# Experts of a large and a small group in alternation, in an encoder trunk on one core

## The chip, the cores and the metric

The kernel runs on 1 core of one Trainium2 chip. The metric is the device time of one execution in microseconds; the median of three runs is 1874.84 us (1874.23 to 1879.55). All computation uses five engines with their own instruction queues: TensorE (PE, matrix products into PSUM), VectorE (DVE), ScalarE (ACT), GpSimd (POOL) and SyncE (SP, which issues the transfers here). An engine takes its instructions strictly in the order in which they stand in its queue.

## The reference

Two layers of an encoder on 512 frames of width 1024. Each layer has a mixer part (retention, differential attention, gated linear attention; not touched here) and then a mixture of experts. The experts are 32 SwiGLU blocks of inner width 512, in 8 groups of 4. A router gives each frame one group and, in it, two experts:

```python
grp = biased.reshape(t, N_GROUPS, EXPERTS_PER_GROUP)
group_score = jnp.sum(lax.top_k(grp, GROUP_SCORE_K)[0], axis=-1)
g_sel = jnp.argmax(group_score, axis=-1)
...
u = jax.nn.silu(xb @ w_gate[e]) * (xb @ w_up[e])
return (u @ w_down[e]) * gts[:, None].astype(xb.dtype)
...
x = x + gt2 * y
```

Everything is float32. The weights of one expert are three matrices of 2 MiB (gate 1024x512, up 1024x512, down 512x1024), so a layer reads 192 MiB of them from HBM.

## The kernel before

The groups are ranked by how many frames chose them. The first four ranks ("wide", `r < NWIDE`) get 128 places each, the last four ("small") 64. All four experts of a group work on all of its places, with gate weights of zero where a frame has not chosen the expert. (Frames that find no place go through a loop behind, which doesn't run for these inputs unless a group overflows.)

Weights come in pieces of 1 MiB (128 partitions x 8 KiB), two to a matrix, issued by SyncE (`fetch`, line 1436) into eight rotating buffers (tag `R8`, names R in the trace; `oldest` picks the place that was used longest ago). A buffer can take its next piece when its last reader is done. What reads it depends on the kind of expert:

- Wide: `split` (line 1407) makes two fp32r halves of each half-piece, ScalarE a rounded copy (`A.copy`, CAST H<-R) and VectorE the rest (`V.tensor_sub`, H<-R,H), into six rotating buffers (tag `H8`, names H). PE multiplies three times per block of the contraction (`three`, line 1417), with 128x128 tiles and 512 columns. The R buffer is free as soon as it is split.
- Small: PE multiplies the float32 piece as it landed (`halved`, line 1421) with 128x64 tiles, and the R buffer stays taken until then.

For expert e the program writes, in this order: the gate product of expert e+1 (`gate_part`; in its middle, `turn` transposes the inner result u of expert e on PE, with ScalarE and VectorE writing the turned copy euT), the down product of e (`down_part`), and the up product of e+1 (`up_part`, whose end is the VectorE multiplication that writes eu). `_Ahead` lets the fetches and splits be written four half-pieces ahead of their use. In this stage every VectorE, ScalarE, GpSimd and TensorE instruction keeps the order in which it is written (`_Pinned`, line 111).

Two further steps belong to a group. `window` (line 1369) makes a wide group's input columns xT (exT) as fp32r pairs, one ScalarE copy and one VectorE subtraction of 128x1024; there is one buffer for it. `combine` (line 1574) adds a finished group's sums to the frames: a mask (ePT) and for each half of the width a gain (eyf), its two fp32r parts (eyh), PE products back to the frame order (x<-eyh,ePT) and a VectorE addition (u<-u,x). It is a generator: `step` (line 1459), called once after each half-piece that PE has multiplied, writes its next portion, so that it runs among the products of later experts. The sums of a wide group take two PSUM banks (tag `y`), those of a small one another bank (tag `y64`, also shown as y in the trace).

What sets the order of the experts is the table `TURNS` (line 35) and the list `where` (line 1588): (rank, number in the group) of the 32 experts; the fetches follow it. Before, the groups come as wholes: the four experts of wide group 0, the four of small group 4, then 1, 5, 2, 6, 3, 7. One variable `ya` holds the sums of the open group.

Of the kernel before, what the change touches and what calls it, by code (L numbers as in the profile page):

```python
# [23 lines left out]
NE, NG, FE = 32, 8, 512  # L24
# [5 lines left out]
NWIDE = 4  # L30
# [1 line left out]
OFFS = tuple(sum(CAPS[:r]) for r in range(NG))  # L32
PLACES = sum(CAPS)

TURNS = (0, 4, 1, 5, 2, 6, 3, 7)


def _constants():
# [100 lines left out]
def hybrid_trunk(ctx: ExitStack, tc: tile.TileContext, x, c, positions, w_mod, b_mod, norm1_g, norm2_g, w_in,  # L139
# [52 lines left out]
    def preload(name):  # L192

        tables[0] = tc.keep_in_program_order(A.preload_act_table_set(name))
# [156 lines left out]
    for l in range(depth):  # L351
        first = l == 0
        with ExitStack() as ps:
# [997 lines left out]
            def pbank(tag, bufs=1, shape=None):  # L1351
                return pm.tile(shape or [128, 512], tag=tag, bufs=bufs)
# [16 lines left out]
            def window(r):  # L1369

                nwin[0] += 1
                xT = wm.tile([128, 2, KD, 128], F32R, tag="exT")
                w = slice(OFFS[r], OFFS[r] + 128)
                for h in ((0, 4), (4, 8)) if nwin[0] == 1 else ((0, 8),):
                    ks = slice(*h)
                    A.copy(xT[:, 0, ks], hs[:, ks, w])
                    V.tensor_sub(xT[:, 1, ks], hs[:, ks, w], xT[:, 0, ks])
                return xT
# [3 lines left out]
            def back(r):  # L1382

                PT = wm.tile([128, NT, 128], F32R, tag="ePT")
                V.tensor_scalar(PT.rearrange("p i t -> p (i t)"), srow, cst("scol")[:, r:r + 1], None, op0=OP.is_equal)
                return PT
# [30 lines left out]
            def three(out, a, ka, hl, c0, start, stop):  # L1417
                for n, (x_, w_) in enumerate(((0, 0), (0, 1), (1, 0))):
                    T.matmul(out, a[:, x_, ka], hl[:, w_, c0:c0 + 512], start=(start and n == 0), stop=(stop and n == 2))

            def halved(out, a, raw, c0, n, start, stop):

                n //= 2
                for h in range(2):
                    T.matmul(out[64 * h:64 * h + 64, 0:n], a, raw[:, c0 + h * n:c0 + (h + 1) * n], start=start, stop=stop)
# [31 lines left out]
            apart = deque()  # L1457

            def step():

                if apart and next(apart[0], apart) is apart:
                    apart.popleft()
# [32 lines left out]
            def turn(u_, e):  # L1495
                b = pbank("x", 3, [128, 4, 128])
                if where[e][0] < NWIDE:
                    for q in range(4):
                        T.transpose(b[:, q], u_.rearrange("p (q t k) -> p q k t", q=2, k=2)[:, q // 2, q % 2], ident)
                    uT = wm.tile([128, 2, 4, 128], F32R, tag="euT")  # L1500
                    A.copy(uT[:, 0], b)
                    V.tensor_sub(uT[:, 1], b, uT[:, 0])
                else:
                    for k in range(2):
                        T.transpose(b[:, k], u_.rearrange("p (t k) -> p k t", k=2)[:, k], ident)
                    uT = wm.tile([128, 2, 128], tag="euT64")
                    A.copy(uT, b[:, 0:2])
                return uT

            def down_part(src, e, uT, ya, amid=None):  # L1510
                r, j = where[e]
                for k in range(4):
                    hl = src.get()
                    start, stop = j == 0 and k == 0, j == 3 and k == 3
                    if r < NWIDE:
                        for n in range(2):
                            three(ya[:, n], uT, k, hl, n * 512, start, stop)
                    else:
                        halved(ya[:, 0], uT[:, k % 2, 64 * (k // 2):64 * (k // 2) + 64], hl, 0, D, start, stop)
                    step()  # L1520
                    if amid and k == 1:
                        amid()

            def gain_y(ya, n, yf, wide_):
                V.tensor_mul(yf, ya[:, n], after["gt2b"][:, n * 512:(n + 1) * 512] if wide_ else after["gt2h"])
                return yf

            def gated(ya, n, wide_):
                return parts(gain_y(ya, n, after["pool"].tile([128, 512], tag="eyf"), wide_))

            def parts(yf):
                yh = after["pool"].tile([128, 2, 512], F32R, tag="eyh", bufs=2)
                A.copy(yh[:, 0], yf)
                V.tensor_sub(yh[:, 1], yf, yh[:, 0])
                return yh

            def store(i, cs_=slice(0, D)):
                SP.dma_start(out[0, i * 128:(i + 1) * 128, cs_], X[:, i, cs_])

            def squares(i, n):  # L1540
                A.activation(wm.tile([128, FE], tag="es"), X[:, i, n * 512:(n + 1) * 512], AF.Square,
                             accum_out=sums[:, i, n:n + 1])

            def add(PT, yhs, ns, i):

                if len(yhs) == 2:
                    bs = [(n, pbank("x", 3), slice(0, 128), yhs[n]) for n in ns]
                else:
                    bs = [(n, pbank("x", 3), slice(64 * n, 64 * n + 64), yhs[0]) for n in ns]
                for m in range(2):  # L1550
                    for n, b, rows, yh in bs:
                        T.matmul(b, PT[rows, i], yh[rows, m], start=(m == 0), stop=(m == 1))
                for n, b, rows, yh in bs:
                    V.tensor_add(X[:, i, n * 512:(n + 1) * 512], X[:, i, n * 512:(n + 1) * 512], b)

            def combine_last(r, ya):

                wide_ = r < NWIDE
                if l + 1 < depth:
                    preload("natural_log_exp_and_others")  # L1560
                PT = back(r)
                yfs = [gain_y(ya, n, wm.tile([128, 512], tag=("es", "eu")[n]), wide_) for n in range(2 if wide_ else 1)]
                yhs = [parts(yf) for yf in yfs]
                for i in range(NT):
                    add(PT, yhs, (0, 1), i)
                    if l + 1 < depth:
                        for n in range(2):
                            squares(i, n)
                    else:
                        store(i)  # L1570
                if l + 1 < depth:
                    row_rstd()

            def combine(r, ya):

                PT = back(r)
                yield
                yhs = []
                for n in range(2 if r < NWIDE else 1):
                    yhs.append(gated(ya, n, r < NWIDE))  # L1580
                    yield
                for ns in ((0,), (1,)) if r < NWIDE else ((0, 1),):
                    for i in range(NT):
                        add(PT, yhs, ns, i)
                        yield


            where = [(r, j) for r in TURNS for j in range(4)]
            ne = len(where)
            items = halves_of(w_gate, 0) + halves_of(w_up, 0)  # L1590
            for e in range(ne):
# [1 line left out]
                mine = halves_of(w_down, e)  # L1593
                items += nxt_[0] + (mine + nxt_[1] if e + 2 < ne else nxt_[1] + mine)
            src = _Ahead(pieces(items), lambda: 4)
            xTs = {TURNS[0]: window(TURNS[0])}

            gh = rt.tile([128, 2, NT, 4], F32R)
            V.tensor_copy(gh[:, 0], gate4)
# [33 lines left out]
            def sums_bank(r):  # L1633
                return pbank("y", 1, [128, 2, 512]) if r < NWIDE else pbank("y64", 1, [128, 1, 512])

            ya = sums_bank(TURNS[0])
            V, A, G, T = [_Pinned(tc, e_) if n_ in "VAGT" else e_ for n_, e_ in
                          (("V", nc.vector), ("A", nc.scalar), ("G", nc.gpsimd), ("T", nc.tensor))]
            turned = []
            for e in range(ne):  # L1640
                r, j = where[e]
                if j == 2 and e + 2 < ne and where[e + 2][0] < NWIDE:
                    xTs[where[e + 2][0]] = window(where[e + 2][0])
                uT = []
                if e + 1 < ne:
                    gacc = gate_part(src, e + 1, lambda: uT.append(turn(u_, e)))
                elif not turned:
                    uT.append(turn(u_, e))
                if e + 2 == ne:

                    u2 = up_part(src, e + 1, gacc)
                    down_part(src, e, uT[0], ya, lambda: turned.append(turn(u2, e + 1)))
                    continue
                down_part(src, e, uT[0] if uT else turned[0], ya)
                if e + 1 < ne:
                    if j == 3:
                        apart.append(combine(r, ya))
                        ya = sums_bank(where[e + 1][0])
                    u_ = up_part(src, e + 1, gacc)
                else:  # L1660
                    combine_last(r, ya)

            V, A, G, T = nc.vector, nc.scalar, nc.gpsimd, nc.tensor
            early = [start_weights(l + 1, r) for r in range(2)] if l + 1 < depth else []
# [6 lines left out]
            with tc.If(nov > 0):  # L1671
# [7 lines left out]
                with tc.For_i(0, NG, 1) as r:  # L1679
                    nb = nc.values_load(nbi[0:1, ds(r, 1)], min_val=0, max_val=NT, skip_runtime_bounds_check_because=bound)  # L1680
                    with tc.If(nb > 0):
# [3 lines left out]
                        with tc.For_i(0, nb, 1) as j_:  # L1685
# [16 lines left out]
                            ya = pbank("y", 1, [128, 2, 512])  # L1702
# [78 lines left out]
```

## Time and profile before

| | |
|---|---|
| median of three runs | 1874.84 us |
| the profiled execution | 1878.26 us |
| its span | 1876.5 us |
| PE busy | 1744.8 us (93%) |
| DVE busy | 1202.0 us (64%) |
| ACT busy | 800.5 us (43%) |
| transfers | 512.05 MB, 273 GB/s in the mean |
| granted TensorE clock, mean over the span | 0.966 of full speed |

The span is the time from the first to the last instruction on the chip; the rest of the execution lies around it. Busy time of PE is modelled at the ends of the products, so a full PE can still be slower than it might be. The two expert stages run about from 464 to 985 us and from 1344 to 1861 us of the span.

### The profile page before, as it was taken

What the parts mean: (1) busy time and instruction counts of PE and PEld (TensorE: products, weight loads), DVE (VectorE), ACT (ScalarE), POOL (GpSimd) and SP (SyncE); (2) the same over time, 40 slices, a digit from 0 to 9 for tenths busy, and PEclk for the clock granted to TensorE, in tenths of its full rate; (3) what the DMA queues carried; (4) which work ended last, traced back from release to release, by engine and by line L of the source; (5) the groups of instructions that cost most, each with busy time, mean ns of one, the idle gap of its engine ahead of it and who ended that gap; (6) DMA issues with size and microseconds to landing.
All of it is one profiled execution on the core that took longest, in us unless ns stands there. A gap on an engine that the chain in (4) does not pass through costs nothing. (4 is left out here: it accounts for less than half of the span.)

```text
span 1876.5 us, 27118 instructions
## 1 busy us (share of the span) xinstructions
PE 1744.8 (93%) x10231; PEld 1286.9 (69%) x10232; DVE 1202.0 (64%) x2062; ACT 800.5 (43%) x1209; POOL 156.2 (8%) x184
## 2 busy tenths in 40 slices
PE   4989899979999999998998999997999899999997
PEld 4866667768865855756748887986885575675663
DVE  6778798665844836728725778657483672872951
ACT  4334343343723714606514555443471561551630
POOL 1233322020000000000000110111000000000000
PEclk9989899998998999999998999998999999999998
DMA  9664556716999989999984211232799999999996
GB/s 287 212 199 126 168 170 216 238 46 242 356 333 424 384 340 423 355 386 423 359 335 149 68 46 46 68 106 89 290 336 354 423 355 381 422 350 389 412 340 271
DMA packets 127831, 512.05 MB, mean 273 GB/s; under 512 B 14942, under 2 KB 59180, under 8 KB 78536
## 3 DMA queue, kind: packets, MB, share of 16 engines
q1 hardware_dynamic: 124168, 504.93, 71.3%
q0 software_dynamic: 1072, 3.32, 0.5%
q10 hardware_dynamic: 2448, 1.94, 0.4%
q8 instruction: 85, 1.39, 0.3%
q14 instruction: 58, 0.48, 0.1%
HBM read 501.72 MB, written 8.42 MB: 272 GB/s over the span
## 5 line engine op out<-in xcount | busy, mean ns | idle before, releaser
L121 DVE TENSOR_TENSOR H<-R,H 128x1024 fp32r<-128x1024 f32 x360 | 421.4, 1220 | 106.8 <-ACT H L121 103.1
L121 ACT CAST H<-R 128x1024 fp32r<-128x1024 f32 x360 | 362.8, 1048 | 100.3 <-DMA R<-in_w_gate_dram 41.8
L582 PE MATMUL a<-H,u 128*128 128x256 f32 x1728 | 249.4, 293 | 0.7 <-DVE P L589 0.7
L582 PEld LDWEIGHTS a<-H,u 128*128 128x128 f32 x1728 | 221.6, 193 | 27.7 <-issue 22.4
L121 PE MATMUL g<-H,exT 128*128 128x512 f32 x720 | 191.6, 413 | 11.0 <-ACT H L121 6.5
L121 PE MATMUL y<-H,euT 128*128 128x512 f32 x768 | 184.9, 396 | 0.0
L121 PE MATMUL u<-H,exT 128*128 128x512 f32 x720 | 178.0, 402 | 0.0
L121 PEld LDWEIGHTS g<-H,exT 128*128 128x128 f32 x720 | 136.7, 195 | 50.2 <-ACT H L121 9.2
L121 PEld LDWEIGHTS y<-H,euT 128*128 128x128 f32 x768 | 143.5, 188 | 37.1 <-ACT H L121 3.1
L121 PEld LDWEIGHTS u<-H,exT 128*128 128x128 f32 x720 | 136.2, 191 | 38.8 <-issue 6.7
L121 DVE SCALAR_TENSOR_TENSOR eu<-u,u,es 128x256 f32<-128x256 f32 (+1 forms) x62 | 37.9, 611 | 180.8 <-PE u L121 180.8
L121 PE MATMUL g<-R,u 128*64 128x256 f32 x1024 | 127.3, 385 | 0.0
L121 PE MATMUL y<-R,euT 128*64 128x512 f32 x512 | 121.8, 600 | 1.1 <-ACT euT L121 1.1
L121 DVE TENSOR_TENSOR u<-u,x 128x512 f32<-128x512 f32 x128 | 85.0, 685 | 59.0 <-PE x L121 58.2
L121 PE MATMUL u<-R,u 128*64 128x256 f32 x1024 | 116.5, 380 | 0.0
L302 DVE SCALAR_TENSOR_TENSOR M<-M,u,M 128x1024 f32<-128x1024 f32 x70 | 97.7, 1395 | 17.0 <-DMA M<-in_w_mod_dram 16.7
L121 ACT COPY euT<-x 128x256 f32<-128x256 f32 x32 | 11.9, 372 | 224.2 <-PE x L121 209.9
L121 PEld LDWEIGHTS u<-R,u 128*64 128x64 f32 x1024 | 72.7, 137 | 48.4 <-issue 15.5
L121 PE MATMUL x<-eyh,ePT 128*128 128x512 f32 (+1 forms) x256 | 80.0, 492 | 21.8 <-ACT eyh L121 17.1
L121 PEld LDWEIGHTS g<-R,u 128*64 128x64 f32 x1024 | 67.8, 136 | 43.2 <-issue 8.7
L121 PEld LDWEIGHTS x<-eyh,ePT 128*128 128x128 f32 (+1 forms) x256 | 33.3, 201 | 75.1 <-DVE u L121 31.0
L121 PEld LDWEIGHTS y<-R,euT 128*64 128x64 f32 x512 | 33.0, 136 | 59.2 <-issue 53.5
(615 smaller groups left out, 2392.7 us busy)
## 6 DMA issues: line engine op xcount, KB each, us to landing
R<-in_w_gate_dram SPq DMA_DIRECT2D x128, 1024.0 KB, 7.6
R<-in_w_up_dram SPq DMA_DIRECT2D x128, 1024.0 KB, 7.5
R<-in_w_down_dram SPq DMA_DIRECT2D x128, 1024.0 KB, 9.5
M<-in_w_mod_dram SPq DMA_DIRECT2D x80, 512.0 KB, 3.9
R<-in_w_in_dram SPq DMA_DIRECT2D x20, 1024.0 KB, 6.4
slab<-in_w_mod_dram SPq DMA_DIRECT2D x16, 512.0 KB
R<-in_w_in_dram SPq DMA_DIRECT2D x24, 256.0 KB, 5.0
R<-in_w_out_dram SPq DMA_DIRECT2D x4, 1024.0 KB
```

The source lines that it names most:

```text
L121: return self.tc.keep_in_program_order(f(*args, **kw))
L302: eng.scalar_tensor_tensor(wm, wm, cc[:, k:k + 1], last, op0=OP.mult, op1=OP.add)
L582: T.matmul(acc[i // 2][:, i % 2], a[q][:, k, tk], hl[:, w, k], start=(i % 2 == 0 and q == 0 and k == 0 and n3 == 0), stop=(i % 2 == 1 and ...
```

## The change

The experts of wide group w and of small group w+4 alternate one by one, with the sums of both groups open at once (`yas`, keyed by rank). The list of the experts is now

(0,0) (4,0) (0,1) (4,1) (0,2) (4,2) (0,3) (4,3) (1,0) (5,0) ... (3,0) (7,0) (3,1) (7,1) (3,2) (3,3) (7,2) (7,3),

the last four being out of the pattern. The window of the next wide group is written two experts ahead of its first expert, as before; there the last expert of the wide group ahead now has its turn. The combination of a wide group is written from the step behind its last expert, and that of the small group one expert later.

```diff
-TURNS = (0, 4, 1, 5, 2, 6, 3, 7)
+WHERE = [(r, j) for w in range(NWIDE) for j in range(4) for r in (w, w + NWIDE)]
+WHERE[-4:] = [(NWIDE - 1, 2), (NWIDE - 1, 3), (NG - 1, 2), (NG - 1, 3)]
...
-            where = [(r, j) for r in TURNS for j in range(4)]
+            where = WHERE
...
-            xTs = {TURNS[0]: window(TURNS[0])}
+            xTs = {where[0][0]: window(where[0][0])}
...
-            ya = sums_bank(TURNS[0])
+            yas = {r: sums_bank(r) for r in (where[0][0], where[1][0])}
...
-                if j == 2 and e + 2 < ne and where[e + 2][0] < NWIDE:
+                if e + 2 < ne and where[e + 2][0] < NWIDE and where[e + 2][1] == 0:
                     xTs[where[e + 2][0]] = window(where[e + 2][0])
...
-                    down_part(src, e, uT[0], ya, lambda: turned.append(turn(u2, e + 1)))
+                    down_part(src, e, uT[0], yas[r], lambda: turned.append(turn(u2, e + 1)))
                     continue
-                down_part(src, e, uT[0] if uT else turned[0], ya)
+                if r not in yas:
+                    yas[r] = sums_bank(r)
+                down_part(src, e, uT[0] if uT else turned[0], yas[r])
                 if e + 1 < ne:
                     if j == 3:
-                        apart.append(combine(r, ya))
-                        ya = sums_bank(where[e + 1][0])
+                        apart.append(combine(r, yas.pop(r)))
                     u_ = up_part(src, e + 1, gacc)
                 else:
-                    combine_last(r, ya)
+                    while apart:
+                        step()
+                    combine_last(r, yas.pop(r))
```

What this does to PE's queue stands at the start of the expert stage of the first layer, behind the first expert's gate and up products (g, u and y are the gate, up and down products, H split weights, R weights as landed, exT a wide group's columns, x with eu the turning of an inner result). Before:

```order
L121 MATMUL g_4517<-H_850_4467,exT_4354 128x512 x6
...
L121 MATMUL x_4538<-u_1_63,eu_4505 128x128 x4
L121 MATMUL g_4517<-H_853_4487,exT_4354 128x512 x6
...
L121 MATMUL y_4516<-H_862_4520,euT_4543 128x512 x6
...
L121 MATMUL u_4617<-H_872_4577,exT_4354 128x512 x6
...
L121 MATMUL g_4660<-H_880_4620,exT_4354 128x512 x6
...
```

The same place of PE's queue after the change:

```order
L122 MATMUL g_4509<-R_849_4465,u_810_4193 64x256 x8
L122 MATMUL x_4526<-u_1_63,eu_4496 128x128 x4
L122 MATMUL g_4509<-R_850_4482,u_810_4193 64x256 x8
L122 MATMUL y_4507<-H_859_4512,euT_4531 128x512 x6
...
L122 MATMUL u_4589<-R_868_4559,u_810_4193 64x256 x8
...
L122 MATMUL g_4624<-H_873_4592,exT_4354 128x512 x6
...
L122 MATMUL y_856_4508<-R_880_4625,euT_882_4642 64x512 x4
...
L122 MATMUL u_4684<-H_885_4660,exT_4354 128x512 x6
```

Where all blocks were of wide experts, every block now is of the other kind than the block ahead of it.

The second place is VectorE's queue where the window of wide group 1 is made (exT), in the first layer. Before, it stands behind the second inner result eu of small group 4:

```order
L121 TENSOR_TENSOR u_672_3591<-u_672_3591,x_5090 128x512
L121 SCALAR_TENSOR_TENSOR eu_5119<-u_5098,u_832_4383,es_5096 128x256
L121 SCALAR_TENSOR_TENSOR eu_5182<-u_5161,u_832_4383,es_5159 128x256
L121 TENSOR_TENSOR exT_5184<-u_810_4193,exT_5184 128x1024
L121 TENSOR_TENSOR H_995_5233<-R_994_5228,H_995_5233 128x1024
```

After the change it stands behind the inner result of the last expert of wide group 0, and the sums of that group (ePT, eyf, eyh) follow among weight rests (H):

```order
L122 SCALAR_TENSOR_TENSOR eu_5107<-u_5078,u_832_4383,es_5076 128x512
L122 TENSOR_TENSOR exT_5109<-u_810_4193,exT_5109 128x1024
L122 TENSOR_TENSOR H_970_5115<-R_969_5113,H_970_5115 128x1024
L122 TENSOR_TENSOR H_971_5122<-R_969_5113,H_971_5122 128x1024
L122 TENSOR_TENSOR euT_5134<-x_5129,euT_5134 128x512
...
L122 TENSOR_TENSOR H_982_5189<-R_981_5184,H_982_5189 128x1024
L122 TENSOR_SCALAR ePT_5196<-u_853_4499,u_1_63 128x512
L122 TENSOR_TENSOR H_984_5198<-R_981_5184,H_984_5198 128x1024
L122 TENSOR_TENSOR eyf_5205<-y_4507,u_866_4550 128x512
L122 TENSOR_TENSOR eyh_5207<-eyf_5205,eyh_5207 128x512
L122 TENSOR_TENSOR H_988_5212<-R_987_5210,H_988_5212 128x1024
```

The window moved from a stretch of small experts to the place between a wide inner result and its turned copy euT, which the wide down product reads; and the sums of a wide group moved in between the rests of the next wide expert's weights.

## Rows read from the trace of the kernel before

**Rows 1.** The page: busy time by engine, and groups of VectorE instructions (busy, mean ns).

```profile
PE 1744.8 (93%) x10231; PEld 1286.9 (69%) x10232; DVE 1202.0 (64%) x2062; ACT 800.5 (43%) x1209; POOL 156.2 (8%) x184
...
L121 DVE TENSOR_TENSOR H<-R,H 128x1024 fp32r<-128x1024 f32 x360 | 421.4, 1220 | 106.8 <-ACT H L121 103.1
...
L121 DVE TENSOR_TENSOR u<-u,x 128x512 f32<-128x512 f32 x128 | 85.0, 685 | 59.0 <-PE x L121 58.2
```

**Rows 2.** Windows: six stretches at small-to-wide borders; length, busy time, clock, transfers.

```profile
577.43:614.87 37.44, 33.39 (x144) 21.00 (x141) 25.75 (x29) 17.94 (x21) 0.00 (x0) 0.86 1.01 423
...
sum 218.33, PE 188.60 PEld 118.62 DVE 151.78 ACT 107.69 POOL 0.00; mean PE 31.43 PEld 19.77 DVE 25.30 ACT 17.95 POOL 0.00
```

**Rows 3.** Timeline of PE, small-to-wide border, layer 2: start, us, tile, [idle before].

```profile
1458.67 3.62 PE L121 MATMUL u<-R,u 128*64 128x256 f32 x32
1463.51 0.50 PE L121 MATMUL g<-H,exT 128*128 128x512 f32 x1 [1.22 <-ACT H L121]
1464.77 4.33 PE L121 MATMUL g<-H,exT 128*128 128x512 f32 x11 [0.76 <-DVE H L121]
...
1472.03 3.65 PE L121 MATMUL y<-R,euT 128*64 128x512 f32 x16
1475.62 4.45 PE L121 MATMUL u<-H,exT 128*128 128x512 f32 x18
1482.44 0.50 PE L121 MATMUL x<-eyh,ePT 64*128 64x512 f32 x2 [2.37 <-ACT eyh L121]
...
1485.18 0.79 PE L121 MATMUL x<-eyh,ePT 64*128 64x512 f32 x4
...
1487.50 0.80 PE L121 MATMUL x<-eyh,ePT 64*128 64x512 f32 x4
```

**Rows 4.** Timeline of ScalarE at the same border.

```profile
1462.41 1.99 ACT L121 CAST H<-R 128x1024 fp32r<-128x1024 f32 x2 [6.58 <-DMA R<-in_w_gate_dram]
```

**Rows 5.** The transfers from 1574 to 1606 us.

```profile
DMA packets 1859, 13.56 MB, mean 424 GB/s; under 512 B 206, under 2 KB 206, under 8 KB 206
```

**Rows 6.** The chain that ended last, among wide experts: start, us, what.

```profile
1357.93 2.79 PE g L121 x12
...
1363.98 5.60 PE y L121 x24
1369.58 5.56 PE u L121 x24
1375.14 2.79 PE g L121 x12
```

**Rows 7.** Timeline of PE, wide-to-small border and the small experts behind.

```profile
1409.48 1.95 PE L121 MATMUL g<-R,u 128*64 128x256 f32 x16
...
1413.91 5.85 PE L121 MATMUL y<-H,euT 128*128 128x512 f32 x24
1419.69 3.67 PE L121 MATMUL u<-R,u 128*64 128x256 f32 x32
1423.29 0.73 PE L121 MATMUL x<-eyh,ePT 128*128 128x512 f32 x2
...
1436.82 3.62 PE L121 MATMUL u<-R,u 128*64 128x256 f32 x32
1440.27 1.90 PE L121 MATMUL g<-R,u 128*64 128x256 f32 x16
...
1444.31 3.60 PE L121 MATMUL y<-R,euT 128*64 128x512 f32 x16
1447.74 3.62 PE L121 MATMUL u<-R,u 128*64 128x256 f32 x32
```

**Rows 8.** By tile exT: VectorE's part; duration min/median/max in ns.

```profile
L121 DVE TENSOR_TENSOR exT<-u,exT x6: 1212/1215/1215, 570.6 to 1714.1; 128x1024 fp32r<-128x1024 f32 x6
```

**Rows 9.** Timeline of VectorE at the wide-to-small border of rows 7.

```profile
1410.33 2.35 DVE L121 TENSOR_TENSOR H<-R,H 128x1024 fp32r<-128x1024 f32 x2
1412.76 0.69 DVE L121 TENSOR_TENSOR euT<-x,euT 128x512 fp32r<-128x512 f32 x1
```

## The prediction

> **What bounds the kernel now.** I read the page first: TensorE (PE) is busy 93% of the span [rows 1], so a change in the order of its work can pay only where it waits or works more slowly than it could. The expert stage of a layer lasts some 517 us and occurs twice. I therefore went to the timeline of PE in that stage. It shows two kinds of expert. A wide one (128 places, split weights, tiles of 128x128) takes 17.21 us, from one gate product at 1357.93 to the next at 1375.14 [rows 6]. A small one (64 places, weights as they land, tiles of 128x64) takes 10.92 us, from one up product at 1436.82 to the next at 1447.74 [rows 7]. The transfers stand against that: when they are not held up they move 13.56 MB in 32 us, 424 GB/s [rows 5], so a piece of 1 MiB (1.049 MB) takes 2.473 us and the six of an expert 14.84 us. A run of four small experts therefore outruns its weights (10.92 against 14.84), and a run of four wide ones leaves the transfers idle in part.
>
> The timeline shows where this is paid: where a small group ends and a wide one begins. PE starts the last up product of the small group at 1458.67 and then stands before the first wide gate product (1.22 us for a ScalarE cast, 0.76 for a VectorE rest) and before the sums of the small group (2.37) [rows 3]. ScalarE, which should cast the weights, has itself waited 6.58 us for the gate weights to land [rows 4]. So the wait that ends last there is the transfer. There are six such places, three in each layer. From the start of that up product to the start of the first wide down product the first of them takes 37.44 us and all six 218.33, with the transfers full (DMA share 1.01) [rows 2].
>
> **What goes.** The same stretch without waits, from rows: small up 3.60 (1419.69 to 1423.29), wide gate 6.05 (1357.93 to 1363.98), small down 3.59 (1472.03 to 1475.62), wide up 5.56 (1369.58 to 1375.14), a second wide gate 6.05, and four steps of the small group's sums at 0.92 each (1485.18 to 1487.50 is 2.32 with the six wide matmuls between, which alone take 5.60 x 6/24 = 1.40): 28.5 us [rows 3, 6, 7]. Six times 28.5 is 171.0; the waits, with the lower clock in some of these stretches (a mean grant of 0.86 in one, so partly 1.2 GHz in place of 2.4) [rows 2], are 218.3 - 171.0 = 47.3 us. In the new order no run of small experts is longer than one (two at the very end), so these six places are gone.
>
> What is late next? A pair of one wide and one small expert needs 12 pieces, 29.68 us of transfers. PE needs 29.01 for it (below), and over a whole round of four pairs another 6.1 for the sums of the wide group (1423.29 to 1436.82 is 13.53, less 4.04 for the gate and 3.43 for the down product inside it) [rows 7] and 3.7 for those of the small one. Between two rounds of sums the transfers thus fall behind by 0.67 us a pair, 2.0 over three pairs. Can the buffers bear this? Before, PE ran from 1436.82 to about 1462.1 through seven small blocks (gate, down or up: 3.64 us each against 4.95 for their two pieces) before it first waited: 1.31 x 7 = 9.2 us of lead used up [rows 3, 7]. Two microseconds against nine, and 9.8 us of sums refill it each round. I cost the transfers at nothing; if the lead were not there, they would cost what the second rival says.
>
> **What is added: changes of kind on PE.** Blocks come as gate of the next expert, down of this one, up of the next. With alternating experts each block is of another kind than the one ahead of it, small, wide, small, wide, six changes to a pair. Where before has such neighbours, the blocks are longer: the small gate 4.43 (1409.48 to 1413.91), the wide down 5.78 against 5.60, the small up 3.60 against 3.45, the small down 3.59 against 3.43 [rows 3, 6, 7]. A pair is then 4.43 + 5.78 + 3.60 + 6.05 + 3.59 + 5.56 = 29.01 us against 17.21 + 10.92 = 28.13 in runs of one kind: 0.88 for six changes, 0.147 each. The new order has 87 changes in a layer (28 experts with three each, and three before the last small pair), the old one 21 (seven borders of groups, three each). 66 more, in two layers 132 x 0.147 = +19.4 us. The pair small up to wide gate was never seen without a wait, so this term has room: 0.1 to 0.2 each, 13 to 26 us.
> The Trainium skill, TensorEngine Tiling (Array Packing), Key Properties, says that a change of tiling mode drains the engine, while a change of tile alone does not; it gives no time. The rows agree in that every border between 128x128 and 128x64 blocks costs 0.1 to 0.2 us, and the sum without the rule would be the third rival.
>
> **What is added: the window.** Before, the 128 columns of the next wide group were cast and their rest taken while small experts ran, on idle engines. Now ScalarE's cast and VectorE's rest (1.21 us) [rows 8] stand right behind the last wide up product and ahead of the weight rests and the turned u that the wide down product waits for. Behind such an up product before, VectorE took two weight rests for 2.35 us from 1410.33, and the rest of the turned u from 1412.76 for 0.69, to 1413.45; PE began the down product at 1413.91, so there was 0.46 of slack [rows 7, 9]. Another 1.21 makes it 0.75 late; if ScalarE's own cast adds to it, up to 2.3. I take 1.0, six times: +6 us (0 to 14). What queues behind it are the weight rests of that down product and of the next gate product, and their cover is the down product itself.
>
> **What is moved: the sums of a wide group.** They ran among small experts, where VectorE had no weight rests. Now two blocks of wide weights fall into the same steps: 8 rests at 1.22 are 9.8 us, 8 additions at 0.685 are 5.5 [rows 1], the mask, products and rests around them some 3.7: 19.0 us, against PE's 3.60 + 6.05 + 3.59 + 6.1 = 19.3. VectorE just keeps up. I take 0.5 us a group, +3 (0 to 12). The sums' matmuls, of 128x128 tiles, now have wide neighbours for five of eight, which may give back some changes of kind: taken as 0, with 6 us either way. SyncE issues the same pieces in another order, and the loads of the group's number are as many; the last two experts are small in both, and their tail stays: 0.
>
> **Sum.** -47.3 + 19.4 + 6 + 3 = -18.9. The profiled execution took 1878.26 us, 1.76 more than its span of 1876.5, so it would be 1859.4; it lies 3.4 above the median of the runs, 1874.84, from which I get 1856. About 0.3% (5.6 us) is what a measurement of this kernel can tell from no change, so up to 1869.2 counts as faster, from 1880.5 as slower.
>
> **Rivals.**
> 1. Slower: the waits before a wide gate product are not the transfer's but the queue's, that is, the casts of a wide block stand in order behind what ScalarE and VectorE do for the small block ahead, and start too late each time. For it: PE waited for cast and rest at every one of the six small-to-wide borders, 1.22 + 0.76 = 1.98 us in the one shown [rows 3]. Against: ScalarE stood idle for the landing just then [rows 4]. The new order has 14 such borders in a layer; 28 x 1.98 = 55 us more, 1911. It decides from 0.87 us a border (24.5 / 28).
> 2. No change: the transfers become the bound and the buffers hold no lead across pairs, so that the sums of a round come on top. For it: a pair wants 29.68 us of transfers for 29.01 of PE, and small pieces keep their buffers until PE has used them. Against: the 9.2 us of lead above. Price: 0.67 x 4 = 2.7 a round, eight rounds, +21: 1877.
> 3. Faster still: changes of kind are hidden because the weight load of the next block runs under the matmuls of the last. For it: the wide gate behind small blocks shows no clear loss. Against: the four longer blocks above. Price: -19, 1837.
> That the scheduler undoes the order isn't one: PE's order alternates as written.
>
> **How the numbers follow.** My forecast 0.62 (1856, own range 1842 to 1870: changes of kind -6 to +7, window -6 to +8, sums -3 to +9, not all at one end), rival 1 0.12, rival 2 0.13, rival 3 0.13. Faster: 0.62 + 0.13, less 0.01 for the upper end, 0.74; same: rival 2 and that end, 0.14; slower: rival 1, 0.12. The range reaches into rivals 2 and 3 and leaves out rival 1: 1835 to 1877.
>
> **What would show it.** Right: no wait of a cast for landing weights longer than a few tenths between small and wide, the clock of PE at 2.4 GHz throughout the stage (granted 1.00), blocks of 4.4, 5.8, 3.6, 6.0, 3.6 and 5.6 us, a wait of about 1 us before the last wide down product of a group (where the window is made), DMA share nearly even at 400 GB/s, and each expert stage about 9.5 us shorter. Wrong: waits of PE for cast or rest at every pair with the transfers below full (rival 1), with the transfers full (rival 2), or blocks as short as in runs of one kind (rival 3).

## The result and the profile after

| | before | after |
|---|---|---|
| median of four runs | 1877.19 us | 1849.07 us |
| profiled execution | 1878.26 us | 1849.14 us |
| first expert stage, start of the first gate product to start of the last down product | 512.96 us | 500.75 us |
| second expert stage | 514.37 us | 500.60 us |

The ratio is 0.9848 (95% interval 0.9814 to 0.9883): 28.1 us faster, where 18.9 were forecast, and 1849 lies in the forecast's own range. The two expert stages give 26.0 of the profile's 29.1 us. The other 3 lie in code that the change doesn't touch: the first stage began 2.9 us earlier, and over the twelve profiles taken here its start varied from 457.2 to 467.8 us.

The page of the changed kernel: PE does the same products in a shorter span, and VectorE as many weight rests as before [rows 1] (eight of them moved from another line of the code).

```profile
span 1847.4 us, 27062 instructions
...
PE 1740.0 (94%) x10231; PEld 1268.4 (69%) x10232; DVE 1197.5 (65%) x2062; ACT 787.6 (43%) x1209; POOL 156.2 (8%) x184
...
L122 DVE TENSOR_TENSOR H<-R,H 128x1024 fp32r<-128x1024 f32 x368 | 430.8, 1220 | 107.4 <-ACT H L122 107.0
```

Windows over the body of both stages and one round (last wide down product of a group to that of the next), of the changed kernel; the columns are the length, busy time of PE, PEld, DVE, ACT and POOL, the granted clock, the DMA share and GB/s:

```profile
464.00:950.00 486.00, 483.06 (x2560) 317.57 (x2559) 298.64 (x319) 216.27 (x265) 0.00 (x0) 1.00 0.98 395
1344.00:1800.00 456.00, 453.21 (x2393) 297.87 (x2394) 283.93 (x302) 207.51 (x253) 0.00 (x0) 1.00 0.98 397
1434.39:1560.92 126.53, 125.60 (x664) 81.46 (x664) 78.50 (x86) 55.79 (x70) 0.00 (x0) 1.00 0.98 397
```

The same windows of the kernel before, and a round of it:

```profile
464.00:950.00 486.00, 472.18 (x2448) 317.75 (x2449) 304.86 (x323) 224.68 (x263) 0.00 (x0) 0.98 0.96 377
1344.00:1800.00 456.00, 440.09 (x2271) 300.07 (x2272) 289.67 (x303) 219.71 (x255) 0.00 (x0) 0.99 0.96 379
1494.77:1626.10 131.33, 125.72 (x665) 82.87 (x665) 79.49 (x86) 57.53 (x69) 0.00 (x0) 0.99 0.97 383
```

PE is now busy for 453 of 456 us, its clock is granted in full (1.00), and the transfers run evenly at 397 GB/s. The timeline of PE after, small to wide and back, answers to [rows 3] and [rows 7]:

```profile
1410.05 3.67 PE L122 MATMUL u<-R,u 128*64 128x256 f32 x32
1413.65 3.07 PE L122 MATMUL g<-H,exT 128*128 128x512 f32 x12
1416.56 0.39 PE L122 MATMUL x<-u,eu 128*128 128x128 f32 x2
1416.71 3.04 PE L122 MATMUL g<-H,exT 128*128 128x512 f32 x12
1419.68 3.65 PE L122 MATMUL y<-R,euT 128*64 128x512 f32 x16
1423.26 5.86 PE L122 MATMUL u<-H,exT 128*128 128x512 f32 x24
1429.05 1.95 PE L122 MATMUL g<-R,u 128*64 128x256 f32 x16
...
1433.49 0.73 PE L122 MATMUL y<-H,euT 128*128 128x512 f32 x2
1434.39 5.40 PE L122 MATMUL y<-H,euT 128*128 128x512 f32 x22 [0.17 <-DVE euT L122]
1439.72 3.67 PE L122 MATMUL u<-R,u 128*64 128x256 f32 x32
```

No wait stands before the wide gate product at 1413.65, where 1.22 and 0.76 us stood before [rows 3]. A block is to be read from its start to the next start: wide gate 6.03, small down 3.58, wide up 5.79, small gate 4.44 (1429.05 to 1433.49); with 5.77 for a wide down product without the window ahead of it and 3.61 for the small up (both from other pairs of the same timeline) a pair takes 29.22, where 29.01 were forecast; nearly all of the difference is the wide up, 5.79 for 5.56. What is left of waits is 0.17 us before the wide down product where the window is made, six times, one of 0.65 at each of six rounds of a small group's sums, and 0.53 at the last expert of each stage.

To settle the terms I summed the blocks of both stages in each timeline, from each start to the next start less the idle time shown (us; "products" are gate, up, down and turning, "sums' products" those of x<-eyh,ePT, "changes" those of kind in one layer; a stage ends here with the start of its last down product; the kernels of the other rows come below):

| kernel | products | sums' products | idle | both stages | changes |
|---|---|---|---|---|---|
| before | 933.9 | 62.6 | 30.8 | 1027.3 | 21 |
| before, half the small transfers | 918.5 | 60.6 | 3.1 | 982.2 | 21 |
| after | 937.2 | 58.0 | 6.2 | 1001.4 | 87 |
| after, half the small transfers | 937.3 | 58.0 | 5.9 | 1001.2 | 87 |
| runs of two | 929.8 | 60.5 | 2.5 | 992.8 | 45 |
| up first | 920.0 | 58.5 | 8.6 | 987.2 | 33 |
| up first, first expert as it was | 920.1 | 58.4 | 4.5 | 983.0 | 35 |

### The profile page after: what moved, and what is told of

Read it like the earlier page. It is cut to its first block, busy times and chain, and to the rows that moved or that the text cites. A ratio compares the mean times of both kernels' runs of the same rounds, so it can differ in the third digit from the quotient of the medians.

```text
span 1847.4 us, 27062 instructions
## 1 busy us (share of the span) xinstructions
PE 1740.0 (94%) x10231; PEld 1268.4 (69%) x10232; DVE 1197.5 (65%) x2062; ACT 787.6 (43%) x1209; POOL 156.2 (8%) x184
## 5 line engine op out<-in xcount | busy, mean ns | idle before, releaser
L122 DVE TENSOR_TENSOR H<-R,H 128x1024 fp32r<-128x1024 f32 x368 | 430.8, 1220 | 107.4 <-ACT H L122 107.0
L122 PE MATMUL g<-H,exT 128*128 128x512 f32 x720 | 183.9, 402 | 0.0
L122 PEld LDWEIGHTS g<-H,exT 128*128 128x128 f32 x720 | 131.5, 188 | 36.1 <-issue 8.5
L122 PE MATMUL x<-eyh,ePT 128*128 128x512 f32 (+1 forms) x256 | 75.1, 459 | 9.1 <-DVE u L122 5.6
L122 ACT CAST euT<-x 128x512 fp32r<-128x512 f32 x32 | 18.7, 584 | 151.0 <-PE x L122 150.8
## 6 DMA issues: line engine op xcount, KB each, us to landing
R<-in_w_down_dram SPq DMA_DIRECT2D x128, 1024.0 KB, 11.7
```

The source lines that it names most:

```text
L122: return self.tc.keep_in_program_order(f(*args, **kw))
```

## The experiments

The theory: the change removes transfer waits of some 47 us at six small-to-wide borders and adds changes of kind on PE. The rivals: the waits were the queues' and not the transfers'; changes of kind cost nothing in sum; the buffers hold no lead in the new order.

**Were the waits for transfers?** The kernel before with small experts fetching half of their weights and using that half twice (it leaves out the other half):

```diff
-                    fetch(raw, wt, expert(r, j), q)
+                    fetch(raw, wt, expert(r, j), q, r >= NWIDE)   # half the rows, into raw[:, 0:1024]
...
-                        half = raw[:, h * 1024:(h + 1) * 1024]
+                        half = raw[:, h * 1024:(h + 1) * 1024] if r < NWIDE else raw[:, 0:1024]
```

> The kernel before, whole groups in turn, with small experts fetching only the first half of each piece (0.5 MiB) and multiplying that half twice: half of the small experts' weights is left out. Theory (the waits at small-to-wide borders are for transfers): six waits of 47 us in sum go, about 1830 us, and the casts of the first wide block find their weights landed. Rival (the casts and rests stand too late in the queues of ScalarE and VectorE): PE still waits about 2 us for H and 2.4 for the sums at each border, and the time stays above 1860.

Measured: 1829.58 us (ratio 0.9757, 0.9709 to 0.9805). Its timeline of PE at the border of [rows 3]:

```profile
1432.54 3.62 PE L121 MATMUL u<-R,u 128*64 128x256 f32 x32
1436.10 3.07 PE L121 MATMUL g<-H,exT 128*128 128x512 f32 x12
...
1442.11 3.65 PE L121 MATMUL y<-R,euT 128*64 128x512 f32 x16
1445.69 4.45 PE L121 MATMUL u<-H,exT 128*128 128x512 f32 x18
1450.08 0.73 PE L121 MATMUL x<-eyh,ePT 64*128 64x512 f32 x4
...
1461.59 5.76 PE L121 MATMUL y<-H,euT 128*128 128x512 f32 x24
```

The same instructions in the same order, and no wait: 29.05 us from the small up product to the wide down product, where before took 36.39 in the mean of [rows 2]. The stages fall from 1027.3 to 982.2, so the waits were worth 45.1 us (47.3 in the prediction): 27.7 of idle time, and 17.4 by which PE's blocks were longer, in stretches where the granted clock was lower (0.86 in the one of [rows 2]). The queue rival falls. This is also the price list of the change: from 982.2 the new order goes up to 1001.4, products +18.7, sums -2.6, idle +3.1.

**Do transfers cost anything in the new order?** The same edit on the changed kernel.

> The changed kernel with small experts fetching only the first half of each piece and using it twice: half of the small experts' weights is left out. Theory (in the changed order the transfers cost PE nothing any more, with eight buffers): no gain, 1849 within 3 us, and the waits of PE for VectorE at the sums (0.65 us in each round) stay. Rival (some of PE's time in the changed kernel still hangs on landing weights): 1835 to 1845.

Measured: 1850.79 us in two runs (1845.78 and 1855.80), stages 1001.2 against 1001.4, the waits of PE the same to 0.3 us. The transfers cost nothing with eight buffers, as the theory has it; the profiled execution is the longer of the two, so what it is longer by lies outside the stages.

**What does a change of kind cost?** Two orders with fewer changes. Runs of two:

```diff
-WHERE = [(r, j) for w in range(NWIDE) for j in range(4) for r in (w, w + NWIDE)]
-WHERE[-4:] = [(NWIDE - 1, 2), (NWIDE - 1, 3), (NG - 1, 2), (NG - 1, 3)]
+WHERE = [(r, j) for w in range(NWIDE) for h in (0, 2) for r in (w, w + NWIDE) for j in (h, h + 1)]
...
-            yas = {r: sums_bank(r) for r in (where[0][0], where[1][0])}
+            yas = {r: sums_bank(r) for r in (where[0][0],)}
```

> The changed kernel with its experts in runs of two: two wide, two small, two wide, two small. Theory (the gain is the transfer waits at the six small-to-wide borders, less about 0.18 us for each change of kind that the rows of the changed kernel show: a pair takes 29.22 us there, 28.13 in runs of one kind, six changes): changes fall from 87 to 45 in a layer, 84 fewer in both, 15 us less than the changed kernel, so some 1834 us; a run of two small experts falls 2 x 3.92 = 7.8 us behind its transfers, less than the 9.2 us of lead seen, so PE meets no new waits. Rival (the lead is shorter when wide and small pieces share the buffers): waits for landing weights come back at the 14 or so small-to-wide borders, some 2 us each, and the time stays at 1849 or rises towards 1860.

Measured: 1840.37 us (ratio 0.9815, 0.9778 to 0.9853), 8.7 less than the changed kernel, not 15. There are no waits for weights (idle 2.5 us), so the lead bears a run of two small experts and the rival is wrong. The products fall by 7.4 us and idle by 3.7, but the sums cost 2.5 more, since those of wide groups stand among small experts again. The products fall by only 0.09 us for each of 84 changes, because the wide gate products rose from 186.4 to 190.7. Most of that rise is no cost of changes of kind, since it lies ahead of the first of them: the first gate product of each stage took 7.4 us here and 5.9 in the changed kernel, and the granted clock fell to 0.50 in it (1.2 GHz; here in the first layer, the columns as above):

```profile
462.00:464.00 2.00, 2.00 (x6) 1.51 (x6) 2.00 (x3) 1.13 (x2) 0.00 (x0) 0.50 0.99 410
```

Why the clock fell there isn't shown. It doesn't belong to this order: the profile with six buffers further down has the same in the first layer alone. Without these 3.1 us the products fall by 10.5, 0.13 a change; without the whole class of wide gate products, in which the small groups' sums now lie, by 11.7, 0.14 a change.

The up product ahead of the down product, so that blocks come in threes of one kind:

```diff
-                items += nxt_[0] + (mine + nxt_[1] if e + 2 < ne else nxt_[1] + mine)
+                items += nxt_[0] + nxt_[1] + mine
...
+                if e + 1 < ne:
+                    u_ = up_part(src, e + 1, gacc)
                 down_part(src, e, uT[0] if uT else turned[0], yas[r])
                 if e + 1 < ne:
                     if j == 3:
                         apart.append(combine(r, yas.pop(r)))
-                    u_ = up_part(src, e + 1, gacc)
```

> The changed kernel, alternating as it is, but with the up product of the next expert ahead of the down product of this one (gate, up, down in place of gate, down, up; the pieces are fetched in that order). Small and wide blocks then come in threes, and a layer has about 31 changes of kind in place of 87. Theory (a change of kind costs PE 0.18 us): 56 x 2 x 0.18 = 20 us less than the changed kernel, about 1829 us. Rival (the longer blocks at borders only show the overlap of one block's end with the next one's start, and nothing is lost in sum): 1849, the same as the changed kernel. A second rival (VectorE can't split three wide blocks in a row in time): PE waits for H and the time is above 1849.

Measured: 1837.34 us (ratio 0.9800, 0.9760 to 0.9840). The expectation said 31 changes; counted in the list of blocks they are 33, so 108 fewer in both layers. Products fall by 17.2 us, 0.16 each (0.14 without the 1.7 us that the window adds to the products of the changed kernel, as shown further down): less than the 0.18 of the theory, but the rival that nothing is lost in sum falls. But there is a new wait, once in each layer, at the first wide down product. PE:

```profile
1340.42 3.62 PE L122 MATMUL u<-R,u 128*64 128x256 f32 x32
1345.27 0.50 PE L122 MATMUL y<-H,euT 128*128 128x512 f32 x1 [1.23 <-ACT H L122]
1346.53 1.65 PE L122 MATMUL y<-H,euT 128*128 128x512 f32 x6 [0.76 <-DVE H L122]
```

And ScalarE at that time, where ACTq is the issue of transfers from ScalarE's queue:

```profile
1338.75 0.59 ACT L122 CAST euT<-x 128x512 fp32r<-128x512 f32 x1 [1.97 <-PE x L122]
1342.36 1.50 ACTq L122 DMA_DIRECT2D u<-u  x3
1343.90 0.38 ACT L122 ACTIVATE es<-g 128x256 f32<-128x256 f32 x1 [4.57 <-issue]
1344.19 9.57 ACT L122 CAST H<-R 128x1024 fp32r<-128x1024 f32 x10
```

The three transfers (the layer's gain) go into the place of the two early weight buffers, and those now held a small expert's up weights, which are free only when PE has used them. ScalarE stood still for 4.57 us around the issue, which in the changed kernel is 0.51, and the casts stood behind it; none of them waited for a landing there. The first expert in its old order (against the variant above):

```diff
-                items += nxt_[0] + nxt_[1] + mine
+                items += nxt_[0] + (nxt_[1] + mine if e else mine + nxt_[1])
...
-                if e + 1 < ne:
+                if e and e + 1 < ne:
                     u_ = up_part(src, e + 1, gacc)
                 down_part(src, e, uT[0] if uT else turned[0], yas[r])
+                if e == 0:
+                    u_ = up_part(src, 1, gacc)
```

> As the variant with gate, up, down in turn, but with the first expert of a layer in the order gate, down, up. There PE waited 1.2 + 0.8 us at the first wide down product of each layer, because ScalarE's queue held the issue of the gain's transfers, which wait for the two early buffers, and these now held a small expert's up weights until PE had used them. Theory: with the wide down weights in those buffers again the wait goes, 2 x 2.0 = 4 us, less 4 changes of kind more, 0.6: 1837 - 3.4 = 1834 us, faster than the changed kernel by some 15. Rival (the wait had another cause, such as the landing of those weights): it stays, 1837.

Measured: 1828.95 us in five runs (1828.36 to 1832.18), ratio to before 0.9743 (0.9717 to 0.9769), where 1834 was expected. The wait is gone and idle falls from 8.6 to 4.5 us, as the theory said; the remaining 4 us between the two medians are not in the stages (983.0 against 987.2) and not explained. It beats both kernels: 46.5 us faster than before, 20 faster than the change. Its blocks, each with one neighbour of its own kind or two (the small gate), are shorter (wide up 5.68, small gate 4.27, small up 3.56, wide down 5.67). The timeline of PE:

```profile
1409.29 5.76 PE L122 MATMUL u<-H,exT 128*128 128x512 f32 x24
1414.97 3.65 PE L122 MATMUL y<-R,euT 128*64 128x512 f32 x16
1418.46 1.90 PE L122 MATMUL g<-R,u 128*64 128x256 f32 x16
...
1422.73 3.62 PE L122 MATMUL u<-R,u 128*64 128x256 f32 x32
1426.29 5.83 PE L122 MATMUL y<-H,euT 128*128 128x512 f32 x24
1431.96 2.95 PE L122 MATMUL g<-H,exT 128*128 128x512 f32 x12
```

**How much lead is there?** The prediction put the lead at 9.2 us and the need at 2. The edit takes buffers of landed weights away: `mr_=4` to `mr_=2` (six in all) or `mr_=3` (seven).

> The changed kernel with six buffers for landed weights in place of eight. Theory (the transfers of a pair fall 0.67 us behind PE, 2 us in a round, and the lead of 9.2 us is what bears it): two pieces fewer are 4.95 us of lead less, 4.2 us remain, still over 2: no new waits of PE, 1849 to 1856 us. Rival (small pieces keep their buffers so long that there is hardly any lead): with six buffers the transfers can't be kept full, PE waits in each pair, 0.5 us or more in each of 32 pairs: over 1865.

Measured: 1876.22 us in eight runs (ratio 1.0010, 0.9987 to 1.0033). The theory is wrong here: six buffers undo the whole gain. PE's new waits come mostly at the rounds of sums (18.9 us for eu and eyh, where with eight buffers there are 0.3), not in each pair as the rival had it. What ScalarE's casts waited for over both stages, in the changed kernel (us in total, times, longest):

```profile
ACT H L122 <- DMA R<-in_w_down_dram: 28.5, 16, 3.8
...
ACT H L122 <- DMA R<-in_w_gate_dram: 9.2, 11, 1.7
```

and with six buffers:

```profile
ACT H L122 <- DMA R<-in_w_gate_dram: 117.9, 41, 5.9
ACT H L122 <- DMA R<-in_w_down_dram: 86.8, 20, 6.4
ACT H L122 <- DMA R<-in_w_up_dram: 52.1, 41, 2.6
```

With eight the casts of the changed kernel already waited for weights 27 times, only PE didn't.

> The changed kernel with seven buffers for landed weights. With eight PE hardly waited, with six the time was 1876, 27 us more. Theory (the lead shrinks evenly and eight is above what the order needs): most of the 27 us come with the sixth buffer gone, so seven give 1850 to 1858. Rival (eight is just at the edge): seven cost half of it or more, 1862 to 1868.

Measured: 1870.93 us in eight runs (ratio 0.9978, 0.9953 to 1.0002). One buffer less costs 22 us of the 27: more than half, as the rival has it, and a little above its range. Its stages take 1021.7 us, summed as in the table, 20.3 more than with eight buffers (1030.2 with six). PE's new waits are mainly at two places. One comes in each round, in the middle of the next wide gate product, 10.3 us in all:

```profile
1463.31 0.50 PE L122 MATMUL x<-u,eu 128*128 128x128 f32 x2 [1.72 <-DVE eu L122]
```

ScalarE and VectorE before it:

```profile
1451.50 2.00 ACT L122 CAST H<-R 128x1024 fp32r<-128x1024 f32 x2 [3.18 <-DMA R<-in_w_gate_dram]
```

```profile
1452.58 1.23 DVE L122 TENSOR_TENSOR H<-R,H 128x1024 fp32r<-128x1024 f32 x1 [2.42 <-ACT H L122]
...
1460.09 0.69 DVE L122 TENSOR_TENSOR eyh<-eyf,eyh 128x512 fp32r<-128x512 f32 x1 [0.69 <-ACT eyh L122]
1461.04 1.23 DVE L122 TENSOR_TENSOR H<-R,H 128x1024 fp32r<-128x1024 f32 x1 [0.26 <-ACT H L122]
1462.18 0.68 DVE L122 TENSOR_TENSOR u<-u,x 128x512 f32<-128x512 f32 x1
1462.78 0.48 DVE L122 SCALAR_TENSOR_TENSOR eu<-u,u,es 128x256 f32<-128x256 f32 x1
```

The gate weights land 3.18 us late for the cast, and VectorE is late with all that stands behind them: rests, the sums of the wide group, and last eu. That is the stretch where the prediction found VectorE just keeping up, so that it can hardly catch up there. The other place is the first wide down product of each stage, 5.1 us in all, where PE waits for euT. Is it the landing? The halved transfers again, now with seven buffers:

> The changed kernel with seven buffers and with small experts fetching only the first half of each piece and using it twice: half of the small experts' weights is left out. With seven buffers the changed kernel took 1871, 22 us more than with eight. Theory (the 22 us are landing times: VectorE's weight rests come late and eu, behind them in its queue, holds PE up by 1.72 us in each round): with less to fetch the waits go, 1847 to 1853. Rival (an odd number of buffers pairs the pieces badly, so that a buffer that a small piece holds blocks the next fetch whatever its size): most of the 22 us stay, over 1862.

Measured: 1857.08 us in two runs (ratio 0.9894, 0.9858 to 0.9930), between the two. The 1.72 us in each round are gone in its timeline, so those were landing times. What stays is 5.5 us at the first wide down product of the two layers (PE for euT, which ScalarE writes), in the first layer with a granted clock of 0.50 behind it. The three transfers are issued just as the small gate product ahead ends, and that is the issue wait shown above, as ScalarE's timeline has it:

```profile
1351.45 1.52 ACTq L122 DMA_DIRECT2D u<-u  x3
1353.01 0.59 ACT L122 CAST euT<-x 128x512 fp32r<-128x512 f32 x1 [3.52 <-issue]
```

With seven buffers and whole transfers it is 3.85 us at the same place. The stages take 1009.7 us, 8.3 above eight buffers. So of the 20.3 us that the eighth buffer is worth in the stages, 12.0 go with the bytes and are landing times; the other 8.3 lie at this issue wait, which the missing buffer has moved to another point of the rotation.

> The variant with gate, up, down from the second expert on (1829 us with eight buffers), with seven. Theory (lead is what counts; three wide and three small blocks in turn need a little more of it than single blocks do, and PE is faster, so the transfers are nearer to their bound): it loses as much as the changed kernel did, 20 to 30 us, 1849 to 1859. Rival (the order of single blocks is what makes buffers short, since each second buffer is held by a small piece): it loses less than 12, under 1841.

Measured: 1852.25 us in two runs (1848.14 and 1856.37; ratio 0.9868, 0.9805 to 0.9931), 23 us more than with eight and inside the theory's range. The stages of the profiled execution, the shorter of the two, take only 15.5 us more, and 5.0 of those are once more PE's wait for euT at the first wide down product, behind the same issue (ScalarE stands for 3.83 us). So the run doesn't say that this order needs more lead than single blocks do.

> The kernel before with six buffers for landed weights in place of eight. Theory (the lead that the buffers hold is what a run of four small experts uses up): two pieces fewer are 4.95 us of lead less at each of six borders, 30 us more: about 1904. Rival (six buffers are short everywhere, since small pieces hold theirs until used, as the changed kernel with six showed): waits inside the small groups too, over 1915.

Measured: 1911.40 us in two runs (ratio 1.0183, 1.0142 to 1.0224), 36 us more than before, between theory and rival: PE's timeline has 42 waits on landing weights inside the small groups, 24.2 us, which the kernel before does not have, and its idle time at the borders, 30 us, is little more than the 27 of before. So here, too, the lead is used up sooner and inside the groups, and not at the borders alone; the rest of the 36 us lies in other waits of PE and in slower products.

## Why the prediction was right

- The waits: 47.3 forecast, 45.1 measured by halving the small experts' transfers. The cause was the landing of weights, as [rows 4] said.
- The changes of kind: +19.4 forecast, +18.7 measured (937.2 - 918.5), 0.142 each where 0.147 were read from the borders of before [rows 3, 6, 7]. The mechanism is borne out, since the products fall with the number of changes in both other orders, by 0.13 to 0.16 a change. That the size came out so near is in part luck. In pairs free of sums a change costs 0.18 (29.22 against 28.13 in runs of one kind, six changes), because the wide up behind a small down takes 5.79 us and not the 5.56 of a run, which would have made +24. Against it, the six wide gate products that sums run through fell from 6.55 to 5.92 us (turning included); the sums among them are now those of a wide group, whose tiles are 128x128 like their own. And 1.7 of the 18.7 belong to the window below.

  The Trainium skill, TensorEngine Tiling (Array Packing), Key Properties, has "Mode switching requires drain", and a loss at each change agrees with it. Tile shape and number format (fp32r or float32) change together at these borders, so the runs don't tell which of them costs the time.
- The window: +6 forecast, +2.8 measured. The term "I take 1.0, six times" was too large. VectorE's queue did what was said, late by 0.8 us:

```profile
1429.23 0.75 DVE L122 SCALAR_TENSOR_TENSOR eu<-u,u,es 128x512 f32<-128x512 f32 x1 [6.25 <-PE u L122]
1430.24 1.23 DVE L122 TENSOR_TENSOR exT<-u,exT 128x1024 fp32r<-128x1024 f32 x1 [0.26 <-ACT exT L122]
1431.38 2.35 DVE L122 TENSOR_TENSOR H<-R,H 128x1024 fp32r<-128x1024 f32 x2
1433.65 0.68 DVE L122 TENSOR_TENSOR euT<-x,euT 128x512 fp32r<-128x512 f32 x1
```

  The rest of the turned u is ready at 1434.33, where PE could have begun at 1433.49. But of the three products with a weight block the first two need only the rounded part, and PE did these two in the meantime: the wait shown is 0.17. The block without it takes 6.06 us where the other wide down products take 5.77, so the window costs 0.46 each time, and 0.29 of that is counted among the products.
- The wide group's sums, +3 forecast for VectorE and 0, with 6 either way, for PE's products among wide ones: PE waits 3.9 us for additions (0.65 in each of six rounds, at the small group's sums behind the wide group's), where in the kernel before with halved transfers it waits 1.5, and the products take 2.6 less. The two products of an addition take 0.47 us from start to start where wide gate parts stand on both sides, among small ones 0.66. So about nothing in sum stands against the +3. Together with the window this is most of what made the change better than forecast.
- The transfers, taken as nothing: right for the time, as the halved transfers show, and wrong in the margin. "2.0 against 9.2" would have borne seven buffers; it did not. The sign "no wait of a cast for landing weights longer than a few tenths" failed too: casts waited 27 times, up to 3.8 us, and PE waited for none of these casts. The 9.2 us were read in a run of small experts that followed a run of wide ones. A likely reason why they don't carry over is that all eight buffers had filled there, while in the alternation small pieces hold theirs until PE has used them and the transfers work at 397 of the 424 GB/s; no run shows this apart. How large the lead is there was not measured, only that one piece less of it (2.47 us) brings 12 us of landing times in two layers.
- The sum: -18.9 forecast. The measured terms are -45.1 + 18.7 - 2.6 + 3.1 (all idle time, 6.2 for 3.1) = -25.9 in the stages, 12.2 and 13.8 us where 9.5 each were forecast. The other 3 us lie outside them, in a start that varies from execution to execution; that they fell on this side is luck.

## What to carry to other kernels

Where work of two kinds has different bounds, interleave it so finely that the buffers bear the difference, and then count what the interleaving itself costs on the bound engine: here two fifths of the gain went into changes of kind, and most of it came back by ordering blocks so that neighbours are of one kind (gate, up, down in place of gate, down, up). A lead that is read from the trace of one order isn't the lead of another: take a buffer away and time it, and look in the trace at what else the missing buffer moved. And see what each queue holds behind an instruction that waits for a buffer; when the order changes, another reader may be the last one to free it.

## What was not expected of the hardware

One buffer of 1 MiB less cost 22 us of 1849, while the next one cost 5 more; and two fifths of the first loss in the stages were not landing times but three transfers whose issue held ScalarE up. And the order of products alone, with the same products and bytes (both kernels with halved transfers), moved the sum of PE's products from 918.5 to 937.3 us.
